# Layer-to-layer transposes of two token tiles at once in the score tiles, and layer two's output gate accumulated ahead of its attention

## The chip, the cores and the metric

The kernel runs on one core of a Trainium2 chip. The metric is the device time of one execution in microseconds (us); three executions of the kernel before took 831.57, 831.68 and 832.28, the median is 831.68.

The engines are TensorE (PE; its weight loads are listed apart as PEld), VectorE (DVE), ScalarE (ACT), GpSimd (POOL) and SyncE (SP), which here only issues DMAs. Each engine works off its own instructions in order and waits for the others by semaphores.

## The reference

A two-layer diffusion backbone in fp32 on 512 latent tokens and 256 context tokens of width 1024. Layer one is differential attention with 8 heads, layer two grouped-query attention with 8 query heads on 2 key/value heads of width 128 and an RMSNorm on each head's q and k. Cut to what matters:

```python
for i in range(2):
    shift, scale, gate = split(silu(c) @ ada_w[i] + ada_b[i], 3)       # context: cshift, cscale, cgate from c_ctx
    h = rms_norm(x, pre_g[i]) * (1 + scale) + shift
    hc = rms_norm(xc, pre_g[i]) * (1 + cscale) + cshift
    # mixer: project to q, k, v, z; rope on latent q, k; latent queries read latent and context keys
    o = softmax(q k^T * dh ** -0.5) v          # layer one: o1 - lam * o2, then rms_norm
    y = (o * silu(z)) @ w_out[i]
    x = x + gate * rms_norm(y, post_g[i])
    # layer one also: xc = xc + cgate * rms_norm(yc, post_g[0])
```

The output is the latent stream x after layer two. Layer two needs no context output, so its q, z and gate are for the 512 latent tokens alone.

## The kernel before, in words

The 768 tokens stand in six tiles of 128: tiles 0 to 3 are latent, 4 and 5 are context. The width of 1024 is eight blocks of 128. Every fp32 product is made as three products of fp32r parts (`mm3`, L147 to L150: high by high, high by low, low by high), so activations and weights exist as a high part, which is a rounded copy (made by ACT), and a low part, the difference (made by DVE or POOL). A weight block of 512 KB is loaded by SP into a buffer of the tag `raw`, of which there are two, then ACT casts it (L211) and POOL or DVE makes the low part (L205).

PSUM has eight banks. Four are the tiles `bk`, handed out in turn: `trp()` gives one for transposes, `pj(n)` gives one that a projection holds until `close`. The other four are two score tiles `sc` of two banks each, handed out by `sc2()`; in attention a unit of scores for 128 queries by 768 keys fills one of them.

Between the layers the work is this. The output product of layer one runs over its third column chunk, 512 wide, tile by tile (loop at L1209): 24 products per tile into a bank. `resid_a` then takes the sum of squares (ACT, L1139) and gates the bank (DVE u, L1169), which frees it. `resid_b` makes the new residual (DVE, L1183), its sums of squares and its inverse root, and POOL writes the normed tile `xn` (L1189; two buffers, tile 4 uses the memory of `gate1`). `h1_tr(m, j)` (L1191) takes one half j of a tile's width: four 128x128 transposes into a bank (L1196), scale and shift from the bank into `hf` (one buffer; two blocks by DVE, L1202, two by ACT, L1204), the rounded copy (ACT, L1206) and the difference (DVE, L1207). The results `h1hi`, `h1lo` are the operands of layer two's projections. Tiles 0 to 3 are transposed inside the loop, two tiles behind the product; tiles 4 and 5 in the next stage.

That next stage makes k and v of layer two in the order of the table `KV`: ('k', m) and ('v', m) are projections of tile m into a bank, ('t', m) transposes tile m of h, ('c', m) transposes a finished k tile (L1264). v is copied and split (L1300, L1301). Then the pool `bp` (with `hf`, `xn` and some weights) is closed, and `t1q` takes its place. `q_proj(p)` projects q for two heads, tile by tile: sum of squares (ACT, L1252), rope (DVE, L1241 and L1243), and transposes later (L1344 is the low part). Attention of layer two runs in 32 units: PE writes scores (L148 to L150), DVE takes the row maxima (L1383) and L1386, ACT the exponentials (L1389, with the row sums), DVE the reciprocal (L1390), POOL the normalization (L219); the probabilities are transposed (L1404), split (ACT L1407, DVE L1408) and multiplied with v. Projections of further q and z tiles are filled in between.

Layer two's output gate is a vector-matrix product for which no tokens are needed: `gate1_part(half, k2)` loads 512 KB of `ada_w` into a `raw` buffer (L1434) and adds two of its 128x512 blocks, each times a column of silu(c), to `gate1` on DVE (L1442 for the first block of a half, L1444 for the rest). After four parts `gate1_finish` sums over partitions with ones on PE and adds bias and post norm's weights (L1452 to L1456). Its ten steps are the stream `Y_` of the planner `flow`, released by the score units 1, 3, 5 and so on to 19.

The order of instructions on each engine is set by a scheduler that goes by the order of the program and by priorities: `hot` raises one, each stream of `flow` has its own, `Y_` has none. `flow` sets the order in which the steps are emitted by due times: a step is due when the steps that it lags behind were emitted plus a delay.

Of the kernel before, what the change touches and what calls it, by code (L numbers as in the profile page):

```python
# [9 lines left out]
F32 = mybir.dt.float32  # L10
F32R = mybir.dt.float32r
AF = mybir.ActivationFunctionType
# [28 lines left out]
TS = 9.0  # L41
HFD = 2
KVE = (0, 1, 0, 1)
KV = (('k', 0), ('k', 1), ('k', 2), ('k', 3), ('t', 4), ('v', 0), ('v', 1), ('k', 4), ('t', 5), ('c', 0), ('k', 5), ('c', 1), ('c', 2), ('c', 3), ('v', 3), ('v', 2), ('v', 5), ('c', 4), ('v', 4), ('c', 5))
SPL = 8.0
GAP0 = 8.0
DL0 = (0.0, 0.0, 0.0, 0.0, 0.0, 0.0, -1.5, 3.0)
# [14 lines left out]
EHL = ('vvvvvvvv', 'pppppppp')  # L62
EWL = 'vppp'
PRI = (1500, 300, 400, 0)
GOFF = 1
GSTEP = 2
QLAG = 4.0
QTR = 2.0
EG0 = 'v'
# [9 lines left out]
def f32(ap):  # L79
    return ap.bitcast(F32)  # L80
# [3 lines left out]
def tile_backbone(  # L84
# [26 lines left out]
    def nm(s):  # L111
        uid[0] += 1
        return f"{s}_{uid[0]}"
# [15 lines left out]
    def trp():  # L129
        i = lru.pop(0)  # L130
        lru.append(i)
        return banks[i]
# [10 lines left out]
    def sc2():  # L143
        scs.append(scs.pop(0))
        return scs[-1]
# [152 lines left out]
    def hot(f, *args):  # L298
        with tc.high_priority(offset=HOT):
            f(*args)  # L300
# [23 lines left out]
    def drain(gen=None):  # L324
        while fillq and (gen is None or gen in fillq):
            ok_ = piece()
            assert ok_ or not fillq or (gen is not None and gen not in fillq)
# [861 lines left out]
        nc.gpsimd.tensor_scalar(t, xd, r, 1.0, ALU.mult, ALU.mult)  # L1189
        xn[m] = t  # L1190

    def h1_tr(m, j):
        v = 0 if m < NQ else 1
        tr = trp()
        for k in range(4):
            nc.tensor.transpose(tr[:, k * P:(k + 1) * P], xn[m][:, (j * 4 + k) * P:(j * 4 + k + 1) * P], ident)  # L1196
        hf = bp.tile([P, 4, P], F32, tag="hf", name=nm("hf"), bufs=1)
        for k in range(4):
            kt = j * 4 + k
            src, s_, h_ = tr[:, k * P:(k + 1) * P], mods[:, 1, v, 1, kt:kt + 1], mods[:, 1, v, 0, kt:kt + 1]  # L1200
            if k < HFD:
                nc.vector.tensor_scalar(hf[:, k, :], src, s_, h_, ALU.mult, ALU.add)  # L1202
            else:
                nc.scalar.activation(hf[:, k, :], src, AF.Identity, scale=s_, bias=h_)  # L1204
        hs = h1hi[:, j * 4:j * 4 + 4, m * P:(m + 1) * P]
        nc.scalar.copy(hs, hf)  # L1206
        nc.vector.tensor_tensor(h1lo[:, j * 4:j * 4 + 4, m * P:(m + 1) * P], hf, f32(hs), ALU.subtract)  # L1207

    for i, m in enumerate(order):  # L1209
        o = pj(n)  # L1210
        run(out_proj(o, ghi, glo, w, m, n, 0, 4))
        if i >= 2:
            h1_tr(order[i - 2], 0)
        run(out_proj(o, ghi, glo, w, m, n, 4, 8))
        resid_a(m, o)
        if i >= 2:
            h1_tr(order[i - 2], 1)
        resid_b(m)
    ws.release(*wout_keys(0, c, n))
    pool_h.close()  # L1220
# [1 line left out]
    with tc.tile_pool(name="t1", bufs=1, side="right") as t1p:  # L1222
# [60 lines left out]
        wv = None  # L1283
        for what, m in KV:
            if what == "t":
                hot(h1_tr, m, 0)
                hot(h1_tr, m, 1)
            elif what == "c":
                k_tr(*ktr.pop(0))
            else:  # L1290
                if what == "v" and wv is None:
                    wv = (ws.get(10), ws.get(11))
                o = pj(256)
                run(proj_tok(o, wk if what == "k" else wv, m))
                if late:
                    k_rope(*late.pop())
                if what == "k":
                    late.append((m, o, head_rstd(o)))
                else:
                    nc.scalar.copy(vh[:, m, :], o)  # L1300
                    nc.vector.tensor_tensor(vl[:, m, :], o, f32(vh[:, m, :]), ALU.subtract)  # L1301
                    close(o)
# [127 lines left out]

        def gate1_part(half, k2):
            acc = gate1[:, half * 512:half * 512 + 512]
            gw = wp.tile([P, 1024], F32, tag="raw", name=nm("raw"), bufs=2)
            nc.sync.dma_start(  # L1434
                gw.rearrange("p (k n) -> p k n", k=2),
                ada_w[1, k2 * 256:(k2 + 1) * 256, 2 * D + half * 512:2 * D + half * 512 + 512].rearrange("(k p) n -> p k n", p=P),
            )
            for k in range(2):
                kt = k2 * 2 + k
                gs = gw[:, k * 512:(k + 1) * 512]  # L1440
                if kt == 0:
                    VP[EGA].tensor_scalar(acc, gs, scol[:, 0, kt:kt + 1], None, ALU.mult)  # L1442
                else:
                    VP[EGA].scalar_tensor_tensor(acc, gs, scol[:, 0, kt:kt + 1], acc, ALU.mult, ALU.add)  # L1444
# [24 lines left out]

        add(q_proj(0))  # L1470
        drain()
        for kind, i in fill1:
            add({"q": q_proj, "z": z1_proj}[kind](i))
        S_, T_, M_, X_ = [], [], [], []
# [15 lines left out]
        for h in range(KT):  # L1490
# [4 lines left out]
            for ch in range(2):  # L1495
# [9 lines left out]
                if h == KT - 1 and ch == 1:  # L1505
                    T_.append(Step(tail1, 0.0, [(M_[-1], 0.0), (u[-1], 0.0)]))
                pv1_steps(h, at, ch, u[-1], T_, M_)
        Y_ = []
        for i in range(10):
            f = (lambda i=i: gate1_part(i // 5, i % 5)) if i % 5 < 4 else (lambda i=i: gate1_finish(i // 5))  # L1510
            Y_.append(Step(f, 0.9 if i % 5 == 4 else 0.0, [(S_[min(31, GOFF + GSTEP * i)], 0.0)], hot=False))
        flow(1, [S_, T_, M_, X_, Y_])
        drain()
        w_o = w_o[0]
# [139 lines left out]
```

## Time and profile before

| | |
|---|---|
| median of three executions | 831.68 us (831.57 to 832.28) |
| profiled execution | 830.24 us |
| its span | 828.4 us |
| mean granted TensorE clock | 0.992 |
| instructions | 14363 |

All lines below are of that one profiled execution, and of core 0. A line of the list of waits reads: engine, tile and source line that waited, then engine, tile and line that it waited for; then the total in us, how often, and the longest. A line of the windows reads: the stretch in us, its length, then busy time and number of instructions of PE, PEld, DVE, ACT and POOL, then the granted TensorE clock as a share of full speed, the DMA engines' busy share and GB/s. A line of the timeline reads: start in us, duration, engine, source line, operation, output tile and input tiles, shape, count, and in brackets the idle time of the engine before it with what ended it. Matmuls are pipelined: their durations overlap, so a product's cost is the distance to the next one's start. "SPq" and "DVEq" are an engine's sequencer. L148 to L150 are the helper `mm3`, L205 to L211 the weight stream; the tile's name tells the use.

### The profile page before, as it was taken

The numbers are of one execution on the slowest core, as the hardware profiler recorded it, in microseconds if no ns is written. First come the engines' busy times: TensorE is split into PE (matmuls) and PEld (weight loads), VectorE is DVE, ScalarE is ACT, GpSimd is POOL, SyncE is SP. The second block draws the span as 40 slices with busy tenths as digits, with TensorE's granted clock in tenths as the row PEclk, the third lists the DMA queues.
The fourth block names the chain that finished last, engine by engine and source line by source line (L and its number), as shares of the span: only waits on it lengthen the run. The fifth ranks groups of instructions, "written<-read, shape, count | busy, mean of one in ns | idle before, by whom it ended". The sixth has DMA issues, their size and how long they took to land. (4 is left out here: it accounts for less than half of the span.)

```text
span 828.4 us, 14363 instructions
## 1 busy us (share of the span) xinstructions
PE 794.2 (96%) x5436; PEld 700.7 (85%) x5436; DVE 483.8 (58%) x909; ACT 456.6 (55%) x997; POOL 435.5 (53%) x612
## 2 busy tenths in 40 slices
PE   7999999999999999999999999889998989999997
PEld 4788897898878898878988898789998879899986
DVE  3745567664767426765278743764266676665634
ACT  5524457564665625855467643754464656666631
POOL 1124847965576752867633203575876746734201
PEclk9999999999999999999999999999999999999999
DMA  9924301212143331414210051121232340301112
GB/s 344 355 72 140 102 14 64 80 63 78 64 122 109 115 99 42 166 57 154 96 51 27 27 204 51 51 85 51 82 101 75 95 155 6 103 26 30 65 34 101
DMA packets 35236, 77.76 MB, mean 94 GB/s; under 512 B 3424, under 2 KB 10336, under 8 KB 35168
## 3 DMA queue, kind: packets, MB, share of 16 engines
q1 hardware_dynamic: 31600, 71.71, 26.0%
q10 hardware_dynamic: 3568, 5.16, 1.8%
q8 instruction: 42, 0.69, 0.4%
q14 instruction: 26, 0.21, 0.1%
HBM read 70.56 MB, written 2.10 MB: 88 GB/s over the span
## 5 line engine op out<-in xcount | busy, mean ns | idle before, releaser
L205 POOL TENSOR_TENSOR wlo<-raw,whi 128x256 fp32r<-128x256 f32 x196 | 148.4, 788 | 117.9 <-ACT whi L211 82.0
L148 PE MATMUL bk<-whi,h 128*128 128x256 f32 (+1 forms) x592 | 177.1, 301 | 5.6 <-DVE u L1169 2.0
L149 PE MATMUL bk<-wlo,h 128*128 128x256 f32 (+1 forms) x592 | 175.9, 298 | 0.3 <-DVE wlo L205 0.3
L150 PE MATMUL bk<-whi,h 128*128 128x256 f32 (+1 forms) x592 | 174.4, 298 | 0.8 <-DVE h L1207 0.8
L148 PE MATMUL bk<-h,whi 128*128 128x512 f32 (+2 forms) x416 | 147.1, 354 | 2.9 <-ACT sq L943 1.5
L149 PE MATMUL bk<-h,whi 128*128 128x512 f32 (+2 forms) x416 | 145.0, 349 | 0.0
L150 PE MATMUL bk<-h,wlo 128*128 128x512 f32 (+2 forms) x416 | 144.8, 349 | 0.0
L148 PEld LDWEIGHTS bk<-whi,h 128*128 128x128 f32 x592 | 112.3, 190 | 15.6 <-issue 3.6
L149 PEld LDWEIGHTS bk<-wlo,h 128*128 128x128 f32 x592 | 112.4, 190 | 4.0 <-DVE wlo L205 0.5
L150 PEld LDWEIGHTS bk<-whi,h 128*128 128x128 f32 x592 | 111.6, 189 | 4.8 <-DVE h L1207 1.2
L219 POOL TENSOR_SCALAR p<-p,sm 128x768 f32<-128x768 f32 (+1 forms) x80 | 67.2, 842 | 67.6 <-DVE sm L1390 23.4
L148 PEld LDWEIGHTS bk<-h,whi 128*128 128x128 f32 x416 | 78.4, 188 | 17.1 <-issue 5.4
L211 ACT CAST whi<-raw 128x1024 fp32r<-128x1024 f32 x64 | 67.3, 1051 | 46.2 <-PE bk L149 15.2
L150 PEld LDWEIGHTS bk<-h,wlo 128*128 128x128 f32 x416 | 78.3, 188 | 8.2 <-issue 1.3
L149 PEld LDWEIGHTS bk<-h,whi 128*128 128x128 f32 x416 | 78.5, 189 | 6.5 <-issue 0.3
L854 ACT ACTIVATE p<-sc,sm 128x768 f32<-128x768 f32 (+1 forms) x68 | 59.6, 880 | 29.7 <-DVE sm L851 29.6
L851 DVE TENSOR_REDUCE sm<-sc 128x1 f32<-128x768 f32 (+1 forms) x68 | 60.6, 918 | 17.0 <-PE sc L846 17.0
L205 POOL TENSOR_TENSOR sz<-sz,za 128x192 f32<-128x192 f32 (+1 forms) x48 | 32.1, 689 | 40.8 <-ACT za L185 40.8
L862 DVE SCALAR_TENSOR_TENSOR p<-p,sm,p 128x768 f32<-128x768 f32 (+1 forms) x34 | 39.0, 1146 | 24.3 <-POOL p L219 23.5
L914 ACT CAST ah<-bk 128x512 fp32r<-128x512 f32 x56 | 31.8, 590 | 31.6 <-PE bk L911 27.3
L915 DVE TENSOR_TENSOR al<-bk,ah 128x512 fp32r<-128x512 f32 x56 | 37.5, 684 | 17.5 <-ACT ah L914 17.3
L846 PE MATMUL sc<-qk,qk 64*128 64x384 f32 (+1 forms) x396 | 46.3, 360 | 1.4 <-ACT p L854 1.4
(236 smaller groups left out, 1683.6 us busy)
## 6 DMA issues: line engine op xcount, KB each, us to landing
raw<-in_a_w SPq DMA_DIRECT2D x28, 512.0 KB, 3.5
araw<-in_ada_w SPq DMA_DIRECT2D x12, 1024.0 KB, 5.3
raw<-in_b_w SPq DMA_DIRECT2D x20, 512.0 KB, 3.5
ag<-in_ada SPq DMA_DIRECT2D x16, 512.0 KB, 7.7
raw<-in_w_out SPq DMA_DIRECT2D x16, 512.0 KB, 3.5
sw<-qr ACTq DMA_DIRECT2D x32, 128.0 KB, 2.1
raw<-in_ada_w SPq DMA_DIRECT2D x8, 512.0 KB, 4.0
xnt<-in_xlT SPq DMA_DIRECT2D x4, 512.0 KB, 5.6
```

Source lines behind the costliest of these rows:

```text
L148: nc.tensor.matmul(o, ahi, bhi, start=start, stop=False)
L149: nc.tensor.matmul(o, ahi, blo, start=False, stop=False)
L150: nc.tensor.matmul(o, alo, bhi, start=False, stop=stop)
L205: eng.tensor_tensor(dst[:, i:i + n], a[:, i:i + n], b[:, i:i + n], op)
L211: nc.scalar.copy(hi, r)
L219: (nc.vector if eng == "v" else nc.gpsimd).tensor_scalar(dst, src, s_, 1.0, ALU.mult, ALU.mult)
L846: prev = nc.tensor.matmul(sc[m][:, j if nk == T else m, :w], a[r, tok], b[r, c], start=i == 0, stop=i == 2)
L851: nc.vector.tensor_reduce(mx, scv, AX.XY if nk == T else AX.X, ALU.max, negate=True)
L854: nc.scalar.activation(pv_, scv, AF.Exp, bias=mx, accum_out=l[:, m:m + 1])
L862: nc.vector.scalar_tensor_tensor(ps_[0], pt, r, ps_[0], ALU.mult, ALU.add)
L914: nc.scalar.copy(ah, tr)
L915: nc.vector.tensor_tensor(al, tr, f32(ah), ALU.subtract)
```

## The change

`h1_tr(p, j)` takes a pair of tiles, 2p and 2p + 1, in place of one tile. Its eight transposes go into one score tile, two banks, not into a `bk` bank. `hf` is 128x4x256 in place of 128x4x128; the scale and shift operations are on 128x256 in place of 128x128, the rounded copy and the difference are made in two halves of 128x2x256. In the loop the calls stand at i = 3 and i = 5 for the pairs 0 and 1, where before there was a call for each tile from i = 2 on. The pair 2, the context, is transposed in the K and V stage, by ('t', 0) and ('t', 1) between the k projections; the rest of the table `KV` has another order.

All eight calls of `gate1_part` are emitted after the first q projection, with tiles `gw` of their own (two buffers in `t1q`) in place of `raw`. Only the two calls of `gate1_finish` stay in the stream `Y_`, released by the score units 6 and 12; before these were 9 and 19. In the changed file the lines of the scores, L147 to L1189, are one lower than before, and those from `h1_tr`'s end on one or two higher.

```diff
--- before.py
+++ after.py
@@ -41,7 +41,7 @@
 TS = 9.0
 HFD = 2
 KVE = (0, 1, 0, 1)
-KV = (('k', 0), ('k', 1), ('k', 2), ('k', 3), ('t', 4), ('v', 0), ('v', 1), ('k', 4), ('t', 5), ('c', 0), ('k', 5), ('c', 1), ('c', 2), ('c', 3), ('v', 3), ('v', 2), ('v', 5), ('c', 4), ('v', 4), ('c', 5))
+KV = (('k', 0), ('k', 1), ('k', 2), ('t', 0), ('k', 3), ('t', 1), ('v', 0), ('v', 1), ('c', 0), ('v', 2), ('c', 1), ('k', 4), ('c', 2), ('k', 5), ('c', 3), ('v', 3), ('v', 4), ('c', 4), ('v', 5), ('c', 5))
 SPL = 8.0
 GAP0 = 8.0
 DL0 = (0.0, 0.0, 0.0, 0.0, 0.0, 0.0, -1.5, 3.0)
@@ -62,8 +62,7 @@
 EHL = ('vvvvvvvv', 'pppppppp')
 EWL = 'vppp'
 PRI = (1500, 300, 400, 0)
-GOFF = 1
-GSTEP = 2
+GFIN = (6, 12)
 QLAG = 4.0
 QTR = 2.0
 EG0 = 'v'
@@ -1189,32 +1188,35 @@
         nc.gpsimd.tensor_scalar(t, xd, r, 1.0, ALU.mult, ALU.mult)
         xn[m] = t
 
-    def h1_tr(m, j):
-        v = 0 if m < NQ else 1
-        tr = trp()
-        for k in range(4):
-            nc.tensor.transpose(tr[:, k * P:(k + 1) * P], xn[m][:, (j * 4 + k) * P:(j * 4 + k + 1) * P], ident)
-        hf = bp.tile([P, 4, P], F32, tag="hf", name=nm("hf"), bufs=1)
+    def h1_tr(p, j):
+        v = 0 if 2 * p < NQ else 1
+        tr = sc2().rearrange("p j (k n) -> p (j k) n", n=2 * P)
+        for i in range(2):
+            for k in range(4):
+                nc.tensor.transpose(tr[:, k, i * P:(i + 1) * P], xn[2 * p + i][:, (j * 4 + k) * P:(j * 4 + k + 1) * P], ident)
+        hf = bp.tile([P, 4, 2 * P], F32, tag="hf", name=nm("hf"), bufs=1)
         for k in range(4):
             kt = j * 4 + k
-            src, s_, h_ = tr[:, k * P:(k + 1) * P], mods[:, 1, v, 1, kt:kt + 1], mods[:, 1, v, 0, kt:kt + 1]
+            s_, h_ = mods[:, 1, v, 1, kt:kt + 1], mods[:, 1, v, 0, kt:kt + 1]
             if k < HFD:
-                nc.vector.tensor_scalar(hf[:, k, :], src, s_, h_, ALU.mult, ALU.add)
+                nc.vector.tensor_scalar(hf[:, k, :], tr[:, k, :], s_, h_, ALU.mult, ALU.add)
             else:
-                nc.scalar.activation(hf[:, k, :], src, AF.Identity, scale=s_, bias=h_)
-        hs = h1hi[:, j * 4:j * 4 + 4, m * P:(m + 1) * P]
-        nc.scalar.copy(hs, hf)
-        nc.vector.tensor_tensor(h1lo[:, j * 4:j * 4 + 4, m * P:(m + 1) * P], hf, f32(hs), ALU.subtract)
+                nc.scalar.activation(hf[:, k, :], tr[:, k, :], AF.Identity, scale=s_, bias=h_)
+        for a in (0, 2):
+            sl = slice(2 * p * P, 2 * p * P + 2 * P)
+            hs = h1hi[:, j * 4 + a:j * 4 + a + 2, sl]
+            nc.scalar.copy(hs, hf[:, a:a + 2])
+            nc.vector.tensor_tensor(h1lo[:, j * 4 + a:j * 4 + a + 2, sl], hf[:, a:a + 2], f32(hs), ALU.subtract)
 
     for i, m in enumerate(order):
         o = pj(n)
         run(out_proj(o, ghi, glo, w, m, n, 0, 4))
-        if i >= 2:
-            h1_tr(order[i - 2], 0)
+        if i in (3, 5):
+            h1_tr(i // 2 - 1, 0)
         run(out_proj(o, ghi, glo, w, m, n, 4, 8))
         resid_a(m, o)
-        if i >= 2:
-            h1_tr(order[i - 2], 1)
+        if i in (3, 5):
+            h1_tr(i // 2 - 1, 1)
         resid_b(m)
     ws.release(*wout_keys(0, c, n))
     pool_h.close()
@@ -1283,8 +1285,7 @@
         wv = None
         for what, m in KV:
             if what == "t":
-                hot(h1_tr, m, 0)
-                hot(h1_tr, m, 1)
+                hot(h1_tr, 2, m)
             elif what == "c":
                 k_tr(*ktr.pop(0))
             else:
@@ -1430,7 +1431,7 @@
 
         def gate1_part(half, k2):
             acc = gate1[:, half * 512:half * 512 + 512]
-            gw = wp.tile([P, 1024], F32, tag="raw", name=nm("raw"), bufs=2)
+            gw = t1q.tile([P, 1024], F32, tag="gw", name=nm("gw"), bufs=2)
             nc.sync.dma_start(
                 gw.rearrange("p (k n) -> p k n", k=2),
                 ada_w[1, k2 * 256:(k2 + 1) * 256, 2 * D + half * 512:2 * D + half * 512 + 512].rearrange("(k p) n -> p k n", p=P),
@@ -1469,6 +1470,8 @@
 
         add(q_proj(0))
         drain()
+        for i in range(8):
+            gate1_part(i // 4, i % 4)
         for kind, i in fill1:
             add({"q": q_proj, "z": z1_proj}[kind](i))
         S_, T_, M_, X_ = [], [], [], []
@@ -1505,10 +1508,7 @@
                 if h == KT - 1 and ch == 1:
                     T_.append(Step(tail1, 0.0, [(M_[-1], 0.0), (u[-1], 0.0)]))
                 pv1_steps(h, at, ch, u[-1], T_, M_)
-        Y_ = []
-        for i in range(10):
-            f = (lambda i=i: gate1_part(i // 5, i % 5)) if i % 5 < 4 else (lambda i=i: gate1_finish(i // 5))
-            Y_.append(Step(f, 0.9 if i % 5 == 4 else 0.0, [(S_[min(31, GOFF + GSTEP * i)], 0.0)], hot=False))
+        Y_ = [Step(lambda i=i: gate1_finish(i), 0.9, [(S_[GFIN[i]], 0.0)], hot=False) for i in range(2)]
         flow(1, [S_, T_, M_, X_, Y_])
         drain()
         w_o = w_o[0]
```

On PE, in the output product of layer one, at the end of tile 3 and the start of tile 4. `bk_68` to `bk_71` are the four one-bank tiles, `sc_72` and `sc_73` the score tiles, `xn_5600` and `xn_5644` the normed tiles 0 and 1. Before:

```order
L148 MATMUL bk_69<-whi_5554,h_5213 128x512
L149 MATMUL bk_69<-wlo_5555,h_5213 128x512
L150 MATMUL bk_69<-whi_5554,h_5214 128x512
L1196 MATMUL bk_71<-ident,xn_5644 128x128 x4
L1196 MATMUL bk_70<-ident,xn_5644 128x128 x4
L148 MATMUL bk_68<-whi_5362,h_5047 128x512
L149 MATMUL bk_68<-wlo_5363,h_5047 128x512
L150 MATMUL bk_68<-whi_5362,h_5048 128x512
```

and now:

```order
L147 MATMUL bk_70<-whi_5554,h_5213 128x512
L148 MATMUL bk_70<-wlo_5555,h_5213 128x512
L149 MATMUL bk_70<-whi_5554,h_5214 128x512
L1196 MATMUL sc_72<-ident,xn_5600 128x128 x3
L1196 MATMUL sc_73<-ident,xn_5644 128x128 x4
L1196 MATMUL sc_72<-ident,xn_5600 128x128
L1196 MATMUL sc_72<-ident,xn_5644 128x128 x4
L147 MATMUL bk_68<-whi_5362,h_5047 128x512
```

Tile 1's transposes stood here alone, in two of the four banks; now tile 0's stand here as well, and all go into the score tiles.

On DVE, in the attention of layer two before, with the score reductions (L1383) and the gate (L1444), whose input is a `raw` tile:

```order
L1383 TENSOR_REDUCE sm_6982<-sc_72 128x1
L1386 TENSOR_TENSOR sm_6984<-sm_6982,qrs_6607 128x1
L1444 SCALAR_TENSOR_TENSOR gate_5296<-raw_6999,scol,gate_5296 128x512 x2
L1390 RECIPROCAL sm_6987<-sm_6987 128x1
L1243 TENSOR_TENSOR tb_6899<-bk_70,ropeb 128x2x64 x2
L1241 TENSOR_TENSOR ta_6964<-bk_69,ropeb 128x256
L1383 TENSOR_REDUCE sm_7060<-sc_73 128x1
L1325 TENSOR_SCALAR qrs_6838<-qrs_6838 128x2
L1444 SCALAR_TENSOR_TENSOR gate_5296<-raw_7132,scol,gate_5296 128x512
L1386 TENSOR_TENSOR sm_7062<-sm_7060,qrs_6487 128x1
L1444 SCALAR_TENSOR_TENSOR gate_5296<-raw_7132,scol,gate_5296 128x512
```

and now up to the first score reduction (L1384), where the gate is L1445 and its input a `gw` tile:

```order
L1445 SCALAR_TENSOR_TENSOR gate_5296<-gw_6630,scol,gate_5296 128x512
L183 SCALAR_TENSOR_TENSOR za_6689<-sz_6687,za_6689 128x512
L1243 TENSOR_TENSOR ta_6731<-bk_68,ropeb 128x256
L1245 TENSOR_TENSOR tb_6732<-bk_68,ropeb 128x2x64 x2
L1445 SCALAR_TENSOR_TENSOR gate_5296<-gw_6630,scol,gate_5296 128x512
L1345 TENSOR_TENSOR ql_6655<-bk_71,qh_6654 128x512
L1345 TENSOR_TENSOR ql_6663<-bk_69,qh_6662 128x512
L1326 TENSOR_SCALAR qrs_6726<-qrs_6726 128x2
L1445 SCALAR_TENSOR_TENSOR gate_5296<-gw_6634,scol,gate_5296 128x512 x2
L1384 TENSOR_REDUCE sm_6749<-sc_73 128x1
L1387 TENSOR_TENSOR sm_6751<-sm_6749,qrs_6457 128x1
```

The gate's operations stood between the reductions of the fourth to the sixth unit and after; now the last of the sixteen, on `gw_6634`, stands ahead of the first reduction, and others between the ropes (L1243, L1245) and the low parts of q (L1345).

On SP, the loads of layer two's weights (`in_b_w`) and of the gate (`in_ada_w`). Before:

```order
L209 DMA raw_6618<-in_b_w 128x1024
L209 DMA raw_6627<-in_b_w 128x1024
L209 DMA raw_6676<-in_b_w 128x1024
L1434 DMA raw_6820<-in_ada_w 128x2x512
L209 DMA raw_6904<-in_b_w 128x1024
L209 DMA raw_6913<-in_b_w 128x1024
L1434 DMA raw_6999<-in_ada_w 128x2x512
L1434 DMA raw_7132<-in_ada_w 128x2x512
L209 DMA raw_7230<-in_b_w 128x1024
L209 DMA raw_7239<-in_b_w 128x1024
L1434 DMA raw_7302<-in_ada_w 128x2x512
L1452 DMA raw_7401<-in_ada_b 128x512
```

and now:

```order
L1435 DMA gw_6606<-in_ada_w 128x2x512
L1435 DMA gw_6610<-in_ada_w 128x2x512
L208 DMA raw_6588<-in_b_w 128x1024
L1435 DMA gw_6614<-in_ada_w 128x2x512
L208 DMA raw_6597<-in_b_w 128x1024
L1435 DMA gw_6618<-in_ada_w 128x2x512
L1435 DMA gw_6622<-in_ada_w 128x2x512
L208 DMA raw_6678<-in_b_w 128x1024
L1435 DMA gw_6626<-in_ada_w 128x2x512
L1435 DMA gw_6630<-in_ada_w 128x2x512
L208 DMA raw_6902<-in_b_w 128x1024
L1435 DMA gw_6634<-in_ada_w 128x2x512
```

The gate's eight loads stood far apart, through the attention; now they are issued in a row with four weight loads among them.

## The prediction

> **What bounds the kernel now.** I read the page first. Its line of busy times names the engine that the rest must feed:
>
> ```profile
> PE 794.2 (96%) x5436; PEld 700.7 (85%) x5436; DVE 483.8 (58%) x909; ACT 456.6 (55%) x997; POOL 435.5 (53%) x612
> ```
>
> TensorE (PE) is busy 794.2 of a span of 828.4 us, and the change takes no product away. What it can win is PE's idle time and time at a lowered clock. So the second view is PE's list of waits, by stage (total, times, longest). From the last part of layer one's output product to the end of layer two's first projections (495 to 600 us):
>
> ```profile
> PE bk L148 <- DVE u L1169: 2.0, 2, 1.3
> PE bk L148 <- ACT hf L1204: 1.1, 3, 0.6
> PE bk L1196 <- DVE u L1169: 0.9, 1, 0.9
> PE bk L150 <- DVE h L1207: 0.8, 2, 0.4
> PE bk L148 <- ACT h L1206: 0.6, 1, 0.6
> PE bk L1264 <- DVE kn L1274: 0.2, 1, 0.2
> ```
>
> These are 5.6 us, and in the largest rows PE wants one of the four one-bank tiles (bk) that the transposes, L1196, share with the projections. Layer two's attention, 580 to 640, 640 to 700 and 700 to 760, in this order:
>
> ```profile
> PE sc L148 <- ACT p L1389: 3.1, 1, 3.1
> ```
>
> ```profile
> PE bk L148 <- ACT sz L1363: 1.6, 1, 1.6
> PE sc L148 <- ACT p L1389: 1.3, 1, 1.3
> PE bk L1404 <- POOL p L219: 0.6, 1, 0.6
> PE bk L148 <- ACT g L1421: 0.2, 1, 0.2
> PE bk L1404 <- DVE al L1408: 0.2, 1, 0.2
> ```
>
> ```profile
> PE sc L148 <- ACT p L1389: 1.6, 1, 1.6
> PE bk L1404 <- ACT g L1421: 0.2, 1, 0.2
> ```
>
> That is 3.1 and 5.7 us. The third view is windows of time: PE, weight loads, DVE, ACT and POOL busy, then the granted clock.
>
> ```profile
> 580.00:600.00 20.00, 20.00 (x148) 18.90 (x147) 5.06 (x17) 8.04 (x23) 17.48 (x28) 1.00 0.24 82
> 624.00:628.00 4.00, 0.91 (x4) 0.81 (x4) 4.00 (x7) 2.16 (x4) 3.54 (x6) 0.92 0.46 143
> 628.00:632.00 4.00, 4.00 (x24) 4.00 (x23) 2.76 (x13) 1.08 (x2) 2.65 (x4) 0.66 0.30 119
> 670.00:674.00 4.00, 3.42 (x27) 3.42 (x28) 2.67 (x5) 3.83 (x9) 3.27 (x4) 1.00 0.16 61
> ```
>
> Behind the 3.1 us stall the granted clock is 0.92 and then 0.66: (0.08 + 0.34) x 4 = 1.7 us of work lost. Round the wait of 1.6 us (670 to 674) it stays 1.00. So the stall at 624 costs 4.8 us, and all waits of these stages together 5.6 + 3.1 + 5.7 + 1.7 = 16.1 us.
>
> The Trainium skill ("TensorE: Matmul & The Clock Gate", Part 1) has the clock fall to half after an idle window of about 3.4 us. By that figure an idle of 3.1 us need not lower it; here it did (0.66), so the measurement decides. By the page alone the forecast below would be 1.7 us higher.
>
> **Part one: two tiles at once in score tiles.** Before, each tile's transposes take one-bank tiles:
>
> ```profile
> 529.15 1.04 PE L1196 MATMUL bk<-ident,xn 128*128 128x128 f32 x8
> 531.11 0.63 PE L1196 MATMUL bk<-ident,xn 128*128 128x128 f32 x4 [0.93 <-DVE u L1169]
> ```
>
> The second row waits for the gating of an earlier tile (L1169) to give its bank back; that gating stands in DVE's queue with the operations that empty the transposes. The score tiles have no user between the layers. With the transposes there, output product and K projections have four banks to themselves, and the three rows that name u (2.0 + 0.9) lose their reason. The 48 transposes stay. The emptying, before, per tile and half:
>
> ```profile
> 518.03 0.73 DVE L1202 TENSOR_SCALAR hf<-bk,mods 128x128 f32<-128x128 f32 x2 [0.69 <-PE bk L1196]
> 518.85 0.81 ACT L1204 ACTIVATE hf<-bk,mods 128x128 f32<-128x128 f32 x2 [2.23 <-DVE hf L1202]
> 520.95 0.69 DVE L1207 TENSOR_TENSOR h<-hf,h 128x512 fp32r<-128x512 f32 x1 [0.69 <-ACT h L1206]
> 578.82 0.41 DVE L1268 TENSOR_TENSOR kl<-bk,kh 128x256 fp32r<-128x256 f32 x1
> ```
>
> An operation on 128x128 takes 0.73/2 = 0.37 on DVE and 0.40 on ACT. On 128x256 it takes between 0.41 (the last row, same size, another operation) and 0.73 (twice the old one); I take 0.47, near the row of the same size. A pair and half then costs DVE 2 x 0.47 in place of 4 x 0.37, 0.5 less, 3 us over six, and ACT about as much. The copies and subtractions keep their size (128x512) and number. This work lies beside PE's products: the first pair beside two tiles of the output product, the second beside k0 and k1. It decides only whether k2 finds its operand. The gain here lies between 0 (each bank wait is followed by an equal one for hf or h) and 5.6. Laying the new order out with the durations above I find one wait of about 0.7 left, a v projection's bank held by the k transposes (kn; the nearest rows are those of 0.2 and 0.6), and take **4.9**.
>
> **Part two: the gate ahead of the attention.** Eight loads of 512 KB and sixteen DVE operations move from among the score reductions to beside layer two's first q projections, into two buffers of their own.
>
> ```profile
> 580.96 0.38 PE L1264 MATMUL bk<-ident,kn 128*128 128x128 f32 x2
> ```
>
> ```profile
> 583.70 12.21 SPq L209 DMA_DIRECT2D raw<-in_b_w  x3
> 598.75 0.38 SPq L1434 DMA_DIRECT2D raw<-in_ada_w  x1
> 604.21 0.80 SPq L209 DMA_DIRECT2D raw<-in_b_w  x2
> ```
>
> ```profile
> 602.81 0.59 DVE L1442 TENSOR_SCALAR gate<-raw,scol 128x512 f32<-128x512 f32 x1 [2.52 <-DMA raw<-in_ada_w]
> ...
> 606.81 0.94 DVE L1383 TENSOR_REDUCE sm<-sc 128x1 f32<-128x768 f32 x1
> ```
>
> ```profile
> L1444 DVE SCALAR_TENSOR_TENSOR gate<-raw,scol,gate x14: 740/752/1368, 603.4 to 680.1; 128x512 f32<-128x512 f32 x14
> ```
>
> The operations are 2 x 0.59 + 14 x 0.75 = 11.7 us of DVE, of which 0.59 + 0.75 already lay ahead of the first reduction. Between 580 and 600 DVE is busy 5.06 of 20 us, so 16 of 20 then: it fits, but the queue is in order, and a gate operation whose load is late holds the q tiles' ropes (L1241, L1243) behind it, and so a PE bank. The first two loads take memory that the last v projection must have left: 580.96 (the k transposes behind it), less 4.9, plus 3 for a q tile now ahead of it (24 products at 20.00/148), near 579. A load takes 602.81 - 598.75 = 4.1 us from issue to use, so the gate starts near 583. Each later load but two waits on SP for the pair before it, or behind a weight load waiting for a raw buffer; the last stands behind the load whose buffer came free at 598.75 before. It is used near 603 and its two operations end by 604.7, and the first reduction starts near 605.6, 1.2 before the old 606.81. In this layout the ropes of the second and the fourth q tile are done 1.2 and 2.0 us before PE wants their banks, and one rope of the next q projection 0.5 to 0.7 after. I charge **0.7**; the bounds are 0 and 3.1 + 1.7 (a stall like the one at 624). Net so far 4.2.
>
> Now the stall. DVE, ACT and PE around it:
>
> ```profile
> 620.77 2.15 DVE L1444 SCALAR_TENSOR_TENSOR gate<-raw,scol,gate 128x512 f32<-128x512 f32 x2 [0.74 <-DMA raw<-in_ada_w]
> 622.84 0.15 DVE L1390 RECIPROCAL sm<-sm 128x1 f32<-128x1 f32 x1
> ...
> 623.63 0.95 DVE L1383 TENSOR_REDUCE sm<-sc 128x1 f32<-128x768 f32 x1
> ...
> 625.28 0.74 DVE L1386 TENSOR_TENSOR sm<-sm,qrs 128x1 f32<-128x1 f32 x1
> ```
>
> ```profile
> 620.95 0.19 ACT L1389 ACTIVATION_READ_ACCUMULATOR p<-sc,sm,qrs 128x1 f32 x1
> ...
> 626.05 0.99 ACT L1389 ACTIVATE p<-sc,sm,qrs 128x768 f32<-128x768 f32 x1 [0.85 <-DVE sm L1386]
> ```
>
> ```profile
> 627.19 0.58 PE L148 MATMUL sc<-kh,qh 128*128 128x384 f32 x1 [3.09 <-ACT p L1389]
> ```
>
> The reciprocal had its sum at 620.95 + 0.19 = 621.14 and ran at 622.84, behind two gate operations: 1.7 late. A third gate operation stands in the order between the reduction and L1386: another 0.75. Without them the exponential at 626.05 starts 2.5 to 3 us earlier, and the 3.1 us wait shrinks to 0.1 to 0.6. But PE now comes 4.2 earlier, the first reduction only 1.2. Some of that difference is taken up by slack: from the end of a score bank's use to its next, PE has other products for 2.8 us or more at every unit, counted in the new order at the 0.135 us of the row 580 to 600. By the layout 0.8 is left at the seventh score unit, too short to lower the clock. So the stall gives 3.1 + 1.7 - 0.8 = **4.0**. I leave the other 5.7 us as they are: the weight loads there lose the gate loads that shared their buffers, but another order of the scheduler stands against that.
>
> Sum: 4.9 - 0.7 + 4.0 = 8.2. The profiled execution took 830.24 (828.4 span and 1.8 around it): 822.0. The median of three runs, 831.68, lies 1.44 higher, so I forecast **823.5**.
>
> **The rivals.**
> *Only the first stretch wins*: PE comes 4.2 earlier to a score chain that cannot, and the stall at 624 comes back with its clock loss. For it: the first reduction moves by only 1.2. Against: 2.5 us of gate work leave just that chain. 831.68 - 4.2 = 827.5.
> *More goes*: DVE has no gate operation between 620 and 690, and half of the other 5.7 us goes too: 820.6; all of it, 817.8. Against: those waits name sz, p and g, on ACT and POOL.
> *Slower: a late gate load.* The last load is issued not at 598.75 but at 604.21, when before the next weight load got its buffer. It is used at 608.3, its two operations end at 609.8, the first reduction is 4.2 later than I have it, PE idles through that (1.7 of clock), and the score chain, no earlier, keeps the 4.0: 823.5 + 4.2 + 1.7 + 4.0 = 833.4, and more by every us that it comes later. It decides from about 5.5 us of delay. For it: SP is in order, and four weight loads stand between gate loads. Against: those waited for buffers that gate loads held, which they no longer do.
> *Nothing*: bank waits turn into hf and rope waits of the same length: about 831.7.
> *Clock loss at the transposes*: twelve now stand in a row, 12 x 1.04/8 = 1.6 us. With a wait of 1.5 us beside them they would reach the 3.1 us after which the clock fell, at 1.7: 825.2. By the rows it takes a wait that the layout does not have. The Trainium skill ("TensorE: Matmul & The Clock Gate", Part 4) says that transposes do not count as PE-busy for the clock as products do; no run here shows that by itself.
>
> **How the numbers follow.** Forecast 0.52 (own range 821 to 826), only the first stretch 0.20, more 0.08, clock loss 0.03, nothing 0.07, slower 0.10. A measurement of this kernel can tell 0.2%, 1.7 us, from no change. Faster is 0.52 + 0.20 + 0.08 + 0.03 = 0.83, the same 0.07, slower 0.10. The range leaves out "nothing" and "slower" (0.17) and the far end of "more": from 819.5, to 829.5, which is the second case with another 2.0 us of waits, what the u rows hold.
>
> **What would show it.** Right: no PE row of bk waiting for u; transposes into sc; PE's waits between 495 and 600 near 1.4 us; no granted clock under 0.9 from 600 on; no row of the gate's accumulation after the first score reduction; that reduction near 605. Wrong: PE or ropes waiting behind gate rows that wait for a load; a wait of PE for p of 3 us or more near unit seven; PE waiting for hf or h before k2; spans that shorten by 4 alone.

## The result and the profile after

The changed kernel took 826.49 us (median of four, 825.61 to 828.16) against 831.98 for the kernel before beside it (831.57 to 833.74): 5.5 us less, a ratio of 0.9942 with a 95% interval of 0.9925 to 0.9959. The forecast was 823.5, within 819.5 to 829.5. The profiled execution took 825.61 us, its span is 823.8; before they were 830.24 and 828.4, so the two traces differ by 4.6 us.

The page's line of busy times shows PE with the same number of instructions:

```profile
PE 792.1 (96%) x5436; PEld 699.6 (85%) x5436; DVE 483.3 (59%) x897; ACT 452.6 (55%) x985; POOL 439.3 (53%) x612
```

PE's waits in the changed kernel, in the stretches used before (495 to 600, 580 to 640, 640 to 700, 700 to 760):

```profile
PE bk L147 <- DVE kn L1276: 1.8, 2, 0.9
PE bk L147 <- DVE vl L1302: 0.7, 1, 0.7
PE bk L1341 <- POOL q L1248: 0.4, 1, 0.4
```

```profile
PE bk L147 <- DVE tb L1245: 2.0, 1, 2.0
PE sc L147 <- ACT qh L1344: 1.5, 1, 1.5
PE bk L147 <- ACT p L1390: 1.2, 1, 1.2
PE bk L1341 <- POOL q L1248: 0.4, 1, 0.4
PE sc L147 <- ACT p L1390: 0.4, 1, 0.4
```

```profile
PE bk L1405 <- DVE al L1409: 1.7, 1, 1.7
PE bk L1405 <- DVE ql L1345: 0.2, 1, 0.2
```

```profile
PE bk L147 <- DVE al L1409: 0.6, 1, 0.6
```

No row waits for u, and the stall of 3.1 us of a score tile on p is down to 0.4. New are 2.0 us on a rope (tb), 1.5 on the first query part (qh) and 1.2 of a bank on p. (The 0.4 on q, at 599.4, stands in two of the lists.) Five windows, one of before and then four of the changed kernel, tell where time was won and where it was given back:

```profile
520.00:540.00 20.00, 17.10 (x88) 13.74 (x87) 14.18 (x24) 15.08 (x36) 12.53 (x22) 1.00 0.17 53
```

```profile
520.00:540.00 20.00, 20.00 (x120) 17.38 (x119) 14.02 (x22) 14.43 (x33) 12.69 (x22) 1.00 0.22 68
580.00:600.00 20.00, 19.56 (x142) 18.23 (x141) 13.06 (x24) 6.82 (x19) 19.48 (x26) 1.00 0.75 242
```

```profile
604.00:608.00 4.00, 2.02 (x12) 1.70 (x12) 4.00 (x8) 0.63 (x1) 3.65 (x5) 0.86 0.75 244
608.00:612.00 4.00, 4.00 (x23) 4.00 (x23) 3.42 (x5) 0.62 (x1) 2.55 (x3) 0.72 0.05 18
```

From 520 to 540 PE is busy all of 20 us in place of 17.10. From 580 to 600 DVE is busy 13.06 in place of 5.06 and the DMA engines move 242 GB/s in place of 82 (the row of before stands in the prediction). From 604 to 612 PE's clock is at 0.86 and 0.72, a loss of (0.14 + 0.28) x 4 = 1.7 us: as large a clock loss as before, 20 us earlier. SP, DVE and PE in that stretch:

```profile
580.33 0.89 SPq L1435 DMA_DIRECT2D gw<-in_ada_w  x2
...
595.70 2.73 SPq L1435 DMA_DIRECT2D gw<-in_ada_w  x2
...
603.82 0.37 SPq L1435 DMA_DIRECT2D gw<-in_ada_w  x1
```

```profile
600.87 1.10 DVE L1445 SCALAR_TENSOR_TENSOR gate<-gw,scol,gate 128x512 f32<-128x512 f32 x1 [2.83 <-DMA gw<-in_ada_w]
...
608.15 2.99 DVE L1445 SCALAR_TENSOR_TENSOR gate<-gw,scol,gate 128x512 f32<-128x512 f32 x2
611.68 0.96 DVE L1384 TENSOR_REDUCE sm<-sc 128x1 f32<-128x768 f32 x1 [0.54 <-PE sc L149]
```

```profile
603.37 0.44 PE L147 MATMUL sc<-kh,qh 128*128 128x384 f32 x1 [1.53 <-ACT qh L1344]
606.32 0.39 PE L147 MATMUL bk<-whi,h 128*128 128x256 f32 x1 [1.99 <-DVE tb L1245]
```

DVE stood 2.83 us waiting for a gate load, with a rope behind it in its queue; the last load was issued at 603.82, and the first score reduction came at 611.68, 4.9 us later than before.

### The profile page after: what moved, and what is told of

It is laid out like the page before. It is cut to its first block, busy times and chain, and to the rows that moved or that the text cites. A ratio compares the mean times of both kernels' runs of the same rounds, so it can differ in the third digit from the quotient of the medians.

```text
span 823.8 us, 14331 instructions
## 1 busy us (share of the span) xinstructions
PE 792.1 (96%) x5436; PEld 699.6 (85%) x5436; DVE 483.3 (59%) x897; ACT 452.6 (55%) x985; POOL 439.3 (53%) x612
## 5 line engine op out<-in xcount | busy, mean ns | idle before, releaser
L147 PE MATMUL bk<-whi,h 128*128 128x256 f32 (+1 forms) x592 | 177.5, 302 | 5.9 <-DVE tb L1245 2.0
L147 PE MATMUL bk<-h,whi 128*128 128x512 f32 (+2 forms) x416 | 147.0, 354 | 3.2 <-ACT sq L942 1.5
L147 PEld LDWEIGHTS bk<-whi,h 128*128 128x128 f32 x592 | 112.9, 191 | 15.5 <-issue 3.6
L147 PEld LDWEIGHTS bk<-h,whi 128*128 128x128 f32 x416 | 78.2, 188 | 17.4 <-issue 5.1
L914 DVE TENSOR_TENSOR al<-bk,ah 128x512 fp32r<-128x512 f32 x56 | 37.4, 683 | 16.9 <-ACT ah L913 16.8
L1409 DVE TENSOR_TENSOR al<-bk,ah 128x512 fp32r<-128x512 f32 x48 | 32.1, 685 | 25.6 <-ACT ah L1408 24.8
```

The source lines that it names most:

```text
L147: nc.tensor.matmul(o, ahi, bhi, start=start, stop=False)
L914: nc.vector.tensor_tensor(al, tr, f32(ah), ALU.subtract)
L1409: nc.vector.tensor_tensor(al, tr, f32(ah), ALU.subtract)
```

## The experiments

Each was timed in five rounds beside the kernel before. The last column but one is DVE's idle time ahead of gate operations until their load landed; the last tells when the first score reduction started. Both are of one traced execution, and three of these were 1.4 to 2.4 us faster than their kernel's median: e3_few_ops (817.97), e7_one_input (821.18) and e10_kv4 (823.55).

| kernel | pairs | gate | us | ratio to before (95%) | DVE idle for gate loads, us | first score reduction |
|---|---|---|---|---|---|---|
| before | no | in the attention, shared buffers | 831.4 to 832.0 | 1 | 9.1 | 606.8 |
| the change | yes | early, own buffers | 826.49 | 0.9942 (0.9925 to 0.9959) | 6.2 | 611.7 |
| the change again | yes | the same | 827.17 | 0.9949 (0.9935 to 0.9962) | 6.0 | 613.2 |
| e1_pair | yes | as before | 835.52 | 1.0051 (1.0038 to 1.0065) | 14.1 | 607.4 |
| e2_gate | no | as in the change | 826.90 | 0.9949 (0.9933 to 0.9966) | 6.6 | 612.8 |
| e4_own_late | yes | own buffers, emitted late | 828.74 | 0.9966 (0.9952 to 0.9979) | 6.9 | 613.1 |
| e13_raw_early | yes | emitted early, shared buffers | 830.67 | 0.9989 (0.9977 to 1.0002) | 6.4 | 606.3 |
| e11_gw1 | yes | as in the change, one buffer | 829.89 | 0.9979 (0.9969 to 0.9990) | 16.1 | 613.1 |
| e10_kv8 | yes | all beside the v projections | 822.18 | 0.9891 (0.9875 to 0.9907) | 0.3 | 608.3 |
| e10_kv4 | yes | half there, half as in the change | 825.83 | 0.9930 (0.9911 to 0.9950) | 2.3 | 610.0 |
| e14_old_kv8 | no | all beside the v projections | 823.97 | 0.9911 (0.9891 to 0.9930) | 1.2 | 610.6 |
| e16_one | yes | the same, one buffer | 829.74 | 0.9971 (0.9959 to 0.9982) | 10.3 | 617.2 |
| e3_few_ops | yes | 12 of 16 operations left out | 819.41 | 0.9851 (0.9838 to 0.9865) | 5.0 | 604.3 |
| e7_one_input | yes | operations with one input | 823.62 | 0.9902 (0.9881 to 0.9924) | 7.2 | 607.9 |

**Each part alone.** For e1_pair the gate went back:

```diff
-        for i in range(8):
-            gate1_part(i // 4, i % 4)
...
-            gw = t1q.tile([P, 1024], F32, tag="gw", name=nm("gw"), bufs=2)
+            gw = wp.tile([P, 1024], F32, tag="raw", name=nm("raw"), bufs=2)
```

and the ten steps of `Y_` as before. Expected:

> Part one alone: the pairs of tiles in the score tiles and the new order of k and v, with the gate as before (raw buffers, released by units 1 to 19). Theory A, the two parts add up: PE's waits between 495 and 600 us fall from 5.6 to about 2.9 as in the changed kernel (gain 3), and the stall on p near the seventh score unit, with its clock loss, stays within 1 us of the 4.8 of before: 828 to 829.5. Theory B, the pairs are the whole gain: 826 to 827. Theory C, PE's earlier arrival is only handed on to the next wait, as the chain of DVE's score reductions sets the time: 831 to 832.

Measured: 835.52, slower than before by 0.5%, more than any theory had. PE's waits from 495 to 600 are the 2.5 us of the changed kernel, so the pairs did what they were to do there. But from 600 to 640 PE waits as follows, and the clock falls further than before:

```profile
PE bk L1406 <- DVE tb L1246: 2.5, 1, 2.5
PE bk L148 <- ACT p L1391: 0.9, 1, 0.9
PE sc L148 <- ACT p L1391: 0.7, 1, 0.7
PE bk L148 <- DVE tb L1246: 0.5, 1, 0.5
```

```profile
624.00:628.00 4.00, 1.77 (x6) 1.37 (x7) 4.00 (x11) 1.79 (x4) 3.82 (x6) 0.70 0.37 132
628.00:632.00 4.00, 4.00 (x17) 3.54 (x16) 4.00 (x12) 1.34 (x3) 2.91 (x4) 0.50 0.41 136
```

On DVE a gate operation stands before a score reduction and waits for its load:

```profile
622.78 0.75 DVE L1446 SCALAR_TENSOR_TENSOR gate<-raw,scol,gate 128x512 f32<-128x512 f32 x1 [2.65 <-DMA raw<-in_ada_w]
```

Before, the first gate operation of that place waited 0.74 us; here 2.65, and it is DVE's queue behind it, ropes and reductions, that PE waits for. So the 3 us won between the layers are handed on and more is lost: theory C's direction, with another price. Why other waits from 640 to 700 grew as well (6.2 us here, 3.9 before, with a clock of 0.67 from 672 to 676) was not taken apart; the scheduler's order differs there too.

e2_gate is the reverse: the old `h1_tr`, loop and table `KV`, with the diff's part on the gate. Expected:

> Part two alone: the gate early with two buffers of its own, the transposes tile by tile in the one-bank tiles and the order of k and v as before. Theory A: the stall near the seventh unit goes (4.8) and so do some of the later waits (about 2 to 3), and 4 to 5 of it is given back by ropes and the first scores behind gate operations: 829 to 830. Theory B: no gain or a loss, 831.5 to 833. Theory C: as PE comes about 3 us later to the late ropes, it waits for them about 3 us less, and the time is that of the changed kernel: 826 to 827.5.

Measured: 826.90, ratio 0.9949. The changed kernel, timed again, gives the same ratio:

> The changed kernel itself once more, in the same company, so that part two alone (ratio 0.9949) can be set against it. If the pairs add nothing to the early gate: ratio to the kernel before 0.993 to 0.996. If they add the 2 to 3 us that they take from the waits between the layers: 0.990 to 0.992.

So with the gate where the change has it the pairs are worth nothing that shows: theory C's number. In e2_gate PE comes later to the late ropes and waits less there, 0.9 on tb and 1.4 on qh and ql, with the clock at 1.00 all through:

```profile
PE sc L149 <- DVE ql L1343: 0.9, 1, 0.9
PE bk L147 <- DVE tb L1242: 0.9, 1, 0.9
PE bk L1339 <- POOL q L1245: 0.5, 1, 0.5
PE sc L147 <- ACT qh L1342: 0.5, 1, 0.5
```

```profile
600.00:620.00 20.00, 17.11 (x127) 16.00 (x126) 14.66 (x30) 10.50 (x25) 18.16 (x23) 1.00 0.44 148
```

**What the early gate gives back.** e3_few_ops leaves DVE operations out and keeps all loads:

```diff
-                else:
+                elif kt == 1:
                     VP[EGA].scalar_tensor_tensor(acc, gs, scol[:, 0, kt:kt + 1], acc, ALU.mult, ALU.add)
```

> The changed kernel with 12 of the 16 gate operations on DVE left out (the blocks 2 to 7 of each half are not added, so layer two's gate is not the reference's); all eight loads stay. If DVE's queue is what holds ropes and first scores: about 13 us of DVE work go, PE's waits between 595 and 612 us fall from 4.0 to under 1, the granted clock stays 1.00 there: 820.5 to 822.5. If it is the loads' time (DVE waiting for data, 242 GB/s in that stretch) or the q weights behind them on SP: the waits keep at least 2.5, 825 to 827.

Measured: 819.41, below either range, and from 600 to 640 PE waits only this:

```profile
PE bk L147 <- DVE tb L1245: 0.6, 1, 0.6
PE sc L147 <- ACT qh L1344: 0.2, 1, 0.2
```

Twelve operations on an engine that is 59% busy cost 7 us: it is DVE's queue ahead of the first scores, not the traffic of the loads, that PE waits for, since from 580 to 600 the DMA engines move 276 GB/s here, more than the 242 of the changed kernel. But without the operations the buffers come free sooner too: the last gate load is issued at 596.56 in place of 603.82. So this run does not part the time of the operations from the lateness of their loads.

e7_one_input sets every gate operation to `tensor_scalar(acc, gs, ...)`, as the first of each half:

> The changed kernel with the 14 operations that read the weights and the sum (two inputs from the state buffer, 1.10 us each) made operations that read the weights alone and overwrite (one input, as the first of each half; so the gate is not the reference's). It measures the slowing by itself. If DVE's and GpSimd's operations with two inputs from the state buffer slow each other: about 0.6 us each with hardly a scatter, GpSimd's weight parts back from 0.93 to about 0.80 us, and with some 7 us less on DVE the time 820 to 823. If the loads' traffic slows every access: 0.8 us or more each, and 824 to 826.

Measured: 823.62. The gate's operations and POOL's weight parts from 580 to 612, in the changed kernel and then in e7_one_input:

```profile
L204 POOL TENSOR_TENSOR wlo<-raw,whi 128x256 fp32r<-128x256 f32 x20 | 18.0, 931 | 0.8 <-ACT whi L210 0.7
L1445 DVE SCALAR_TENSOR_TENSOR gate<-gw,scol,gate 128x512 f32<-128x512 f32 x14 | 15.3, 1096 | 3.9 <-DMA gw<-in_ada_w 3.7
```

```profile
L204 POOL TENSOR_TENSOR wlo<-raw,whi 128x256 fp32r<-128x256 f32 x20 | 15.4, 802 | 1.6 <-ACT whi L210 1.6
L1443 DVE TENSOR_SCALAR gate<-gw,scol 128x512 f32<-128x512 f32 x16 | 11.7, 730 | 7.5 <-DMA gw<-in_ada_w 7.2
```

The answer is between the two theories. POOL's parts go back to 0.80 us, so the two-input operations did slow POOL; but the one-input operations, at 0.73 against 0.48 for the fastest, are slowed as well. That two inputs alone are the reason is not shown.

**Buffers or place in the program.** e4_own_late keeps `gw` and puts all parts back in `Y_`; e13_raw_early keeps the early calls and puts `gw` back in `raw`:

> The changed kernel with the gate's parts back in the attention (released by units 1 to 19 as before), but with its own two buffers in place of those of the weight stream. It tells the place of the operations from the sharing of buffers. If the sharing cost before (weight loads waiting behind gate loads, gate operations waiting for them): faster than part one alone by 1 to 3 us, 825.5 to 827.5, and no late stall near the seventh unit. If the place of the gate operations among the reductions was the cost: within 1 us of part one alone, 828 to 829.5, with a stall of 2 us or more on p.

> The changed kernel with its gate loads in the weight stream's two buffers, as before, but emitted right after the first q projection: the pairs, the early emission, no buffers of its own. In DVE's order the gate's sixteen operations then reach from the fourth q rope to behind the third score reduction. If the own buffers are what makes the gate early and the gain: 829 to 833, as the gate is among the reductions again and PE waits 3 us or more for p or for late weights. If the emission ahead of the attention is enough: 825.5 to 828.

In e4_own_late DVE's thirty-six instructions from the first gate operation to the first score reduction are those of the changed kernel, in the same order, all sixteen gate operations among them: with late calls the scheduler still took them as early, so here the buffers decided. So neither reading of that expectation could be tested; what it shows is that the own buffers alone bring the whole gate ahead of the first reduction (828.74; the sums over partitions come later). e13_raw_early shows the other half: with shared buffers the early calls do move the gate, its last operation starts at 622.09 in place of 680.10, but ten of the sixteen still stand between the first reduction and the fourth, and at 830.67, with an interval that holds 1, nothing is won that shows.

**The gate moved further.** e10_kv8 defines `gate1_part` ahead of the k and v stage, takes `gw` from `bp` and calls it there:

```diff
+        gp = [0]
         for what, m in KV:
+            for _ in range({('v', 0): 2, ('v', 1): 1, ('v', 2): 1, ('c', 1): 1, ('c', 2): 1, ('c', 3): 1, ('v', 4): 1}.get((what, m), 0)):
+                gate1_part(bp, gp[0] // 4, gp[0] % 4)
+                gp[0] += 1
```

> The changed kernel with all eight gate parts moved earlier still, to beside the v projections (two buffers in the memory of the stage between the layers). Theory D: what the changed kernel gives back (waits of 3.5 us for ropes and q parts between 600 and 608 us and 1.7 of clock) comes from crowding 16.6 us of gate operations, slowed beside POOL, into DVE's queue between 584 and 611; beside the v projections DVE is busy 6 of 20 us, so first reduction near 604 to 606, PE waits between 595 and 612 under 1, clock 1.00: 819.5 to 822. Rival, the gate operations now hold kn and vl, and PE waits for its banks there instead (2.5 us there now becomes 5 or more): 825 to 828.

Measured: 822.18, 4 to 5 us better than the change and the best of all kernels with the whole computation. PE's waits from 495 to 560 and from 560 to 600 did grow, to 6.5 us, as the rival had it:

```profile
PE sc L1196 <- POOL xn L1188: 1.2, 1, 1.2
PE bk L149 <- DVE h L1209: 1.1, 1, 1.1
```

```profile
PE bk L147 <- DVE vl L1321: 1.9, 2, 1.3
PE bk L1266 <- POOL kr L1248: 1.3, 1, 1.3
PE bk L149 <- DVE h L1209: 0.6, 1, 0.6
PE bk L149 <- POOL wlo L204: 0.4, 1, 0.4
```

but none is longer than 1.3 us, the clock stays at 1.00, and from 600 on only 1.8 us of waits are left. The loads are no longer late; the first two were issued near 485, almost 60 us ahead of their use:

```profile
L1298 DVE SCALAR_TENSOR_TENSOR gate<-gw,scol,gate 128x512 f32<-128x512 f32 x14 | 12.3, 880 | 0.4 <-DMA gw<-in_ada_w 0.3
```

The first reduction, at 608.3, was not at the 604 to 606 that I had made its mark, and PE did not wait for it.

e10_kv4 moves half of the parts, e14_old_kv8 all of them in the old kernel:

> Half of it: the first four gate parts beside the v projections, the other four where the change has them. Theory D: half the crowding, about half to all of the gain of the full move, 820.5 to 824. Rival: 825 to 828.

> The old transposes tile by tile in the one-bank tiles, with the eight gate parts beside the v projections. Together with the full move it tells what the pairs are worth where the gate no longer crowds DVE. If the pairs are worth what they take from PE's waits between the layers: 2.5 to 3.5 us slower than the full move with pairs, 823 to 825. If PE's earlier arrival is handed on to later waits whatever stands there: within 1 us of it.

825.83 for half lies in the rival's range, and its interval overlaps that of the change. In its traced execution two stretches have a clock loss (560 to 580 and 600 to 620, 0.91 each); the second stands behind one wait:

```profile
PE bk L147 <- ACT za L180: 1.9, 1, 1.9
```

```profile
600.00:604.00 4.00, 3.08 (x16) 3.11 (x17) 3.62 (x6) 1.67 (x3) 3.84 (x5) 0.67 0.40 133
```

e14_old_kv8 took 823.97, 1.8 us more than with pairs, in the range of the first reading. But its interval, 0.9891 to 0.9930, overlaps that of e10_kv8, and its gate calls stand at other places of the table `KV`, so whether the pairs pay once the gate is out of the way stays open.

**One buffer.** Two tries to space the operations by a single `gw` buffer, at the v projections and at the change's place:

> The full move beside the v projections with one buffer for the gate's loads in place of two, so that each load waits for the two operations before it: in DVE's order the operations then stand apart, from the first k projections to the first ropes of q. Theory D, crowding: PE's waits between 540 and 600 us, 6.5 with two buffers, fall to about 3 to 4, nothing new later: 819 to 821.5. Rival: the last pairs reach into the q projections and hold ropes again, 822 to 825.

> The changed kernel with one buffer for the gate's loads in place of two, at the change's place: the operations reach from the q ropes to the fifth score reduction. If crowding ahead of the first reduction is what gives time back: waits for ropes and q parts between 595 and 612 fall from 3.5 to 1 or less, 822 to 825. If a gate operation among the first reductions costs as much as before: 826 to 829.

Both failed, 829.74 and 829.89. A single buffer does space the operations in the order, but each load then starts only when the operations before it are done, and DVE stands waiting. In e16_one the v tiles' low parts stand behind such an operation, and PE's bank behind them:

```profile
PE bk L147 <- DVE vl L1321: 5.7, 2, 3.4
```

```profile
L1298 DVE SCALAR_TENSOR_TENSOR gate<-gw,scol,gate 128x512 f32<-128x512 f32 x14 | 12.7, 908 | 8.4 <-DMA gw<-in_ada_w 8.3
```

This corrects theory D: the crowd of operations is not all that costs, a late load at the head of an in-order queue does too. The column of idle times goes with the column of times only roughly: 0.3 to 2.3 us for the three kernels at 822 to 826, 6 to 7 for those at 826 to 831, 9 to 16 for those at 830 to 836, and in this last group 16.1 us go with 829.89 and 14.1 with 835.52. Nor is it the loads alone. e3_few_ops and e7_one_input, with shorter work for DVE, are 3 to 7 us faster than the change at about its idle time (5.0 and 7.2), and in e10_kv8, with its loads on time, PE's waits between the layers still grew from 2.5 to 6.5 us. How much of the loss is each one's was not parted.

## Why the prediction was right, and where it was not

The direction and the range held, and 5.5 of the forecast 8.2 us came. That is in part luck: 826.49 is outside the narrower range of the forecast's own case (821 to 826), the rope term came out eight times its size, and a gain that the sum put at nothing made up for much of it. Both kernels are at the same point up to 516.7 us (0.05 apart), so what follows arose behind it. Term by term, in the traces:

- *Between the layers, forecast 4.9.* The 5.6 us of bank waits, all but 0.2 of them on u, hf and h, went; 1.8 on kn and 0.7 on vl are left: 3.1 won. I had one wait of 0.7 left, on kn; two of 0.9 on kn came, and one of 0.7 on vl that I did not see. Operations on 128x256 took 0.99 us for two, 0.50 each (0.47 assumed).
- *Ropes behind gate operations, forecast -0.7.* This is the step that failed: 2.0 on tb, 1.5 on qh, 0.4 on q and 1.7 of clock are 5.6, above the bound of 4.8 that I had set. I took 0.75 us for a gate operation, the median among the reductions; beside a busy POOL they took 1.10 on average and 16.6 in all, not 11.7. And I had the last load issued near 599, behind a weight load; the weight load did go at 598.66, but the gate load behind it waited until 603.82 for DVE to be done with one of the two gate buffers. The first reduction came at 611.68, not 605.6.
- *The stall at 624, forecast 4.0.* 4.8 went, 1.2 and 0.4 came: 3.2.
- *Later waits, forecast 0.* 5.7 became 2.5: 3.2 won. In e2_gate, without the pairs, 0.9 are left there: gate operations between the reductions had cost there too. The rows named ACT for p, but the exponential itself waits for DVE (the row of 626.05 in the prediction).

3.1 - 5.6 + 3.2 + 3.2 = 3.9 of the 4.6 between the traces; the rest lies in no wait that the lists show.

Of the signs that I had named, three of the right ones came as said (no bank waits for u, transposes into sc, no gate accumulation after the first reduction), and three did not: PE's waits from 495 to 600 are 2.9 us, not 1.4, the clock is under 0.9 behind 600, and the reduction is late. One of the wrong ones came: ropes behind gate rows that wait for a load. In number the result is nearer to the rival *only the first stretch wins* (827.5) than to 823.5, but its account is not what happened: the stall at 624 did not come back, and e1_pair and e2_gate give the gain to the gate.

The rival of the late gate load had its time right within 0.4 us: last load issued at 604.21 (603.82), used at 608.3 (608.15). That was luck, for it had the load wait behind a weight load, and it waited for a gate buffer. Its price was wrong: I had added the stall at 624 to it, and the delay of the first reductions came in that stall's place. I read this as a queue that, late once, is not late again for the same work; no run shows that by itself. "It decides from about 5.5 us of delay" failed with it: the reduction was 6.1 us later than in my layout and the kernel was still faster.

That the two parts add up was an assumption of the sum, and e1_pair and e2_gate refute it: the pairs alone cost 4.0 us, the gate alone gives all of the gain. In e2_gate PE loses 2.8 us round the late ropes, in the changed kernel 5.6 with the clock, a difference of about what the pairs had won; so I read those 3 us as an earlier arrival at DVE's queue. The Trainium skill ("TensorE: Matmul & The Clock Gate", Part 1) puts the idle window before the clock falls at about 3.4 us. Here it fell after 1.53 and 1.99 us with about 1 us of products between, and in e10_kv4 to 0.67 from 600 to 604 behind a single wait of 1.93. Before, a wait of 1.6 left it at 1.00, and so did one of 1.95 in e7_one_input (at 625.66). The measurement decides: a sum that charges the clock only from 3 us on is too low in this kernel, and the length of one wait does not tell whether the clock falls.

## What to carry to other kernels

When two parts of a change each take a wait from the busiest engine, check whether the second wait ends on the same queue: time won ahead of an in-order queue that is itself late is handed on to the next wait, so such terms need not add. Filler work for an idle vector engine is priced by its load as well as by its own time: put it where its data has landed long before, since one operation that waits for a DMA holds all behind it. And give it buffers that let its loads run ahead; with them the scheduler here put the work at the same place whether its calls came early or late.

## What the runs showed of the hardware

- DVE's two-input operations on 128x512 took 0.73 to 1.65 us in the changed kernel, 1.10 on average from 580 to 612 (POOL was busy 19.48 of 20 us from 580 to 600); POOL's weight parts took 0.93 there, against 0.74 in the same stretch before:

```profile
L205 POOL TENSOR_TENSOR wlo<-raw,whi 128x256 fp32r<-128x256 f32 x20 | 14.1, 736 | 6.5 <-ACT whi L211 6.5
```

- The granted clock fell after two idle times that were each under 2 us (603.37 and 606.32) to 0.86 and 0.72, as much as after the single one of 3.1 before.
